# Zero-state products left out, a padded tile, stacked low-rank halves and a relaid instruction list in a three-branch decoder trunk

## Chip, cores and metric

The kernel runs on one core of one Trainium2 chip. The metric is the device time of one execution in microseconds (us), the median of several. Before the change three runs took 2274.77 to 2276.88 us, with a median of 2276.57 us.

## What is computed

A decoder trunk with 2 layers, a width of 1024 and 1024 tokens, in float32. Each layer makes one wide input projection, feeds three token mixers from it (pooling, retention, RWKV-7), projects each mixer's output, merges the three by gates, and projects once more:

```python
def hybrid_layer(x, c_act, positions, ...):
    mod = c_act @ w_ada + b_ada
    shift, scale, gate = jnp.split(mod[:, None, :], 3, axis=-1)
    h = rms_norm(x, norm_g) * (1.0 + scale) + shift
    proj = h @ w_in
    ...
    o_pool = causal_pool_mixer(pool_u, pool_w, pool_scale) * jax.nn.silu(pool_g)
    o_ret = retention(q, k, v, positions, ret_norm_g) * jax.nn.silu(ret_g)
    o_rwkv = rwkv7_time_mix(rw, ...) * jax.nn.silu(rw_g)
    branches = jnp.stack([o_pool, o_ret, o_rwkv], axis=2)
    y = jnp.einsum('btnw,nwd->btnd', branches, w_branch)
    gates = jax.nn.sigmoid(gate_logits.reshape(B, T, N_BRANCHES, D))
    merged = jnp.sum(gates * y, axis=2)
    return x + gate * (merged @ w_out)
```

Two mixers carry a state that starts at zero, and both need two low-rank or recurrent steps that matter here:

```python
def rwkv7_time_mix(p, shift_mu, w0, w2, a0, a2, ...):
    ...
    w = -jax.nn.softplus(-(w0 + jnp.tanh(wl) @ w2)) - 0.5
    a = jax.nn.sigmoid(a0 + al @ a2)
    ...
    def step(S, inp):
        r_t, w_t, k_t, v_t, a_t, b_t = inp
        sa = jnp.einsum('bhvk,bhk->bhv', S, a_t)
        S = (S * w_t[:, :, None, :] + sa[..., None] * b_t[:, :, None, :]
             + v_t[..., None] * k_t[:, :, None, :])
        return S, jnp.einsum('bhvk,bhk->bhv', S, r_t)
    _, y = lax.scan(step, jnp.zeros((B, H, N, N), jnp.float32), xs)

def retention(q, k, v, positions, ret_norm_g):
    ...
    def step(R, kv_n):
        return chunk_decay * R + kv_n, R
    _, R_prev = lax.scan(step, jnp.zeros((B, H, dh, dh), jnp.float32), jnp.moveaxis(kv, 2, 0))
```

Here `wl` and `al` are 64 wide and `w2`, `a2` are 64x512.

## The kernel before

All activations lie with channels on the 128 partitions and tokens along the free dimension, in two halves `h` of 512 tokens. A projection tile of 128 channels is 8 blocks of contraction. Each float32 operand is split into a high part that the fast matmul type (F32R) holds exactly and the low rest, and each block is three products: high times high, high times low, low times high (`mm1`). These products, 128x128 weights by 512 columns, go to PSUM tiles named `acc` and make up most of the program; I call them ordinary products. Plain float32 products (state, scores, transposes) are issued in two passes, transposes in one.

**The RWKV mixer** (`rwkv_task`) runs once per layer and pair of heads: 8 tasks, one after the other. A task treats 1024 tokens as 16 chunks of 64. `prepare` makes the scaled keys and queries for each half. It begins with the low-rank products (`lora_mm`, PSUM tiles `lw`): `tanh(wl) @ w2` uses partitions 0 to 63 of both operands and `al @ a2` partitions 64 to 127, each as three products of a high and a low part, so six products over 64 rows each. Their weights `lw` are loaded and split once per layer (`lora_load`), their moving operands `lt` once per half by the evacuation of the `lora` item (`evac_`). `scores` transposes the keys of each chunk (`bt` to `BKt`) and makes the score blocks `G` (PSUM tiles `g` and `two`); `states` makes `AV` (PSUM tile `av`); `invert` and `blocks` invert the unit triangular parts on DVE and in 32x32 products (`m1`, printed as `m`, and `two`). Then the loop over 16 chunks runs, and each step depends on the one before:

1. `two<-S,AR`: the state times the chunk's queries and keys; DVE adds `AV` and writes `xst`; ACT scales the state to `SP`.
2. `ch<-xst,G`: two products with 64 columns of data; the weight is 65 columns of `G`, where the last unit of the tile has only 64 left. ACT copies the result to `Z`.
3. `ch<-Z,BKt`: the update; DVE forms the next state `Sn` from it and `SP`, 64x64 per head.
4. `two<-Z,G`: the chunk's output, copied to `y` by ACT.

**The retention mixer** (`ret_task`) runs once per layer and head: 8 tasks of two halves, each with 4 blocks of 128 tokens. It makes scores (`rs`), transposes keys and values (`rkt`, `rvt`), makes the block products (`rkv`) and from them on DVE the running state `R`, and the output (`ro`).

**The order.** The program is not issued as it is written. Every call is recorded (`Log.call`), with a lane and a place; `Log.plan` then lays out a list for each engine. It goes through time, takes the engine that is free first, and among the operations that are ready by then the one with the smallest key (the place in the recording plus a bias per lane; RWKV has -3000). `pe_time` and `times` give each operation's length, and a few constants the extra length on PE: `SWITCH` (86 ns) when an ordinary product follows another kind, and `RESHAPE` (100 ns) when the rows of the weight or the half of output partitions differ from the product before. A tile of a ring of buffers is handed out in the order of the recording. `nc.emit` issues the list, so every instruction in the profile has the one line L543, and groups are told apart by their tiles. TensorE (PE), DVE, ACT, POOL (GpSimd) and SP's DMA queue each run their list in order.

Of the kernel before, what the change touches and what calls it, by code (L numbers as in the profile page):

```python
# [111 lines left out]
HOLD = 3000  # L112
SWITCH = 86
SEED = 0
SHAKE = 0
SIDE = 0.6
RESHAPE = 100
RATE = 0.0027
# [86 lines left out]
class Log:  # L205
# [75 lines left out]
    def pe_time(self, n, a, k):  # L281
        out = a[0]
        w = a[1] if n == "transpose" else k["lhsT"]
        f = out.free_size()
        if n != "transpose" and k["rhs"].dtype == F32R:
            t = 228 if f > 256 else 120
        else:
            t = 426 if f == 1 else (max(f * 0.846, w.free_size() * 0.8) + 3) * (1 if n == "transpose" else 2)
        return t / 2 if w.partition_size() == 64 and out.partition_size() == P else t

    def times(self, o):
        o.port = False
        n = max(x.free_size() for x in o.outs + o.ins_)
        if o.eng == "PE":
            occ = sum(self.pe_time(q, a, k) for _, a, k, q in o.calls)
# [41 lines left out]
    def plan(self):  # L337
# [102 lines left out]
        burst = None  # L440
        spell, was, shape = 0, False, None
        while len(done) < len(todo):
# [114 lines left out]
def trunk_kernel(ctx, tc, xT, cvec, pos, vecs, consts, w_ada, w_all, pool_w, lora_w, out):  # L557
# [7 lines left out]
    wp = pool("wp", 2)  # L565
    gp = pool("gp", 1)
    rp = pool("rp", 4)
    tp = pool("tp", 4)
    mp = pool("mp", 4)
    sb = pool("sb", 1)  # L570
# [8 lines left out]
    def gtile(s):  # L579
        return gp.tile([P, 32 * P], F32, tag="G", name=nm(s))  # L580

# [629 lines left out]
    def ret_task(l, hd, qT, kT, vT, sg):  # L1211
# [6 lines left out]
        for h in range(2):  # L1218
# [14 lines left out]
            kt = mo("rkt")  # L1233
            nc.scalar.activation(kt, ps, AF.Copy, scale=tl)
            yield 900
# [10 lines left out]
            with nc.together():  # L1246
                for c in range(4):
                    mmul(cl(kv, c), lhsT=cl(kt, c), rhs=cl(vt, c), start=True, stop=True)
            R = []
            for c in range(4):  # L1250
                R.append(prev)
                nx = sb.tile([P, P], F32, tag="R", name=nm("R"), bufs=4)
# [35 lines left out]
    def rwkv_task(l, hp, kT, rT, vp, lt, lw):  # L1288
        hc = slice(hp * P, (hp + 1) * P)
# [3 lines left out]
        G = Gf.rearrange("p (u n) -> p u n", n=P)  # L1293
        qa = lambda b: slice(64 + 32 * b, 96 + 32 * b)
# [8 lines left out]
        def prepare(h):  # L1303
            cr = slice(8 * h, 8 * h + 8)
            yield wait(*lt[h])
            pss = [mx("lw"), mx("lw")]
            lora_mm(pss, lw, hc, lt[h])
            sg = t_ri("sg")
# [84 lines left out]
        def scores(h):  # L1393
            yield max(until(whole[h] + 1000), wait(Z, spare=600))
            for q in range(2):
                ps = mx("bt")
                c0 = 8 * h + 4 * q
                with nc.together():
                    for c in range(4):
                        trans(ps[:, c * P : (c + 1) * P], jt(BK, slice(0, P), c0 + c), timed=True)  # L1400
                nc.scalar.copy(BKt[:, c0 : c0 + 4, :], ps.rearrange("p (c n) -> p c n", n=P))
                yield 1300
# [114 lines left out]
        for c in range(16):  # L1517
# [4 lines left out]
            S, Sn = SS[par], SS[1 - par]  # L1522
            pcc = pc[:, c : c + 1]
            SP = sb.tile([P, P], F32, tag="SP", name=nm("SP"), bufs=1)
            nc.scalar.activation(SP, S, AF.Copy, scale=pcc)
# [5 lines left out]
            if c > 1:  # L1531
                sa.own_dep = yout[-2]
            nc.vector.tensor_tensor(xst[0:64, :], cy[64:128, 0:P], AV[:, c * P : (c + 1) * P], op=ALU.add)
# [10 lines left out]
            for hd in range(2):  # L1544
                rw = slice(64 * hd, 64 * hd + 64)
                nc.vector.scalar_tensor_tensor(
                    Sn[rw, rw], ch[rw, P + 64 * hd : P + 64 * hd + 64], pc[rw, c : c + 1], SP[rw, rw],
                    op0=ALU.mult, op1=ALU.add,
                )
            yield 500  # L1550
            for hd in range(2):
# [4 lines left out]
                    Z[:, c, cols],  # L1556
                    start=False,
                    skip_group_check=True,
# [54 lines left out]
    def enter_layer(l):  # L1613
        nonlocal L_
        rope[:] = [None, None, None]
        L_ = (l, {}, {}, [])
        L_[3].extend(lora_load(l))

    def lora_load(l):
        raw = wp.tile([P, W], F32, tag="wr", name=nm("lraw"), bufs=3)  # L1620
        nc.sync.dma_start(out=raw, in_=lora_w[l])
        lw = [cp.tile([P, W], F32R, tag=f"lw{j}", name=nm("lw")) for j in range(2)]
        split(raw, *lw, nc.vector)
        return lw
# [10 lines left out]
    def evac_(item, ps, h):  # L1635
        l, st, ams, lw = L_
        kind = item[0]
        if kind == "lora":
# [4 lines left out]
            st.setdefault("lt", [None, None])[h] = r  # L1643
            split(d, *r, nc.vector)
        elif kind in ("k", "r", "v"):
# [8 lines left out]
            if kind == "v" and h == 1:  # L1654
                st[("task", i)] = rwkv_task(l, i, st[("k", i)], st[("r", i)], st[("v", i)], st["lt"], lw)
                add("rwkv", st[("task", i)])
# [263 lines left out]
    add("st", store_all([(hd[0][kt, h], xin[h][kt]) for h in range(2) for kt in range(8)]))  # L1920
    L_ = (0, {}, {}, [])
    L_[3].extend(lora_load(0))
    for i in range(3):
# [376 lines left out]
def _pack(inputs):  # L2300
# [78 lines left out]
    arr["pool_w"] = np.ascontiguousarray(f("pool_w"))  # L2379
    arr["lora_w"] = np.ascontiguousarray(np.concatenate([f("rwkv_w2"), f("rwkv_a2")], axis=1))  # L2380
    return arr
# [22 lines left out]
```

## Time and profile before

| What | Value |
|---|---|
| timed runs | 2274.77, 2276.57, 2276.88 us |
| median | 2276.57 us |
| span of the profiled execution | 2272.5 us |
| PE matmul instructions | 13076 |
| DVE, ACT, POOL instructions | 2776, 1795, 552 |
| mean DMA rate | 110 GB/s |

The span is the profiled execution's own time, from its first to its last instruction; the timed runs also hold what lies around it. How to read the rows in the prediction: in a list by time the first two numbers are start and length in us, "out<-in" are tiles by name, "128*65" are the rows and columns of the weight in use, "128x512" the result, and "x4" the number of instructions merged in the row. A matmul's length is its way through the array and not the time that it takes from the next one, so the distance between starts is what counts. In group rows the numbers behind the bar are busy us and mean ns of one, then the idle time before. In rows of one tile, three numbers are the shortest, median and longest ns of one.

### The profile page before, as it was taken

The numbers are of one execution on the slowest core, as the hardware profiler recorded it, in microseconds if no ns is written. First come the engines' busy times: TensorE is split into PE (matmuls) and PEld (weight loads), VectorE is DVE, ScalarE is ACT, GpSimd is POOL, SyncE is SP. The second block draws the span as 40 slices with busy tenths as digits, with TensorE's granted clock in tenths as the row PEclk, the third lists the DMA queues.
The fourth block names the chain that finished last, engine by engine and source line by source line (L and its number), as shares of the span: only waits on it lengthen the run. The fifth ranks groups of instructions, "written<-read, shape, count | busy, mean of one in ns | idle before, by whom it ended". The sixth has DMA issues, their size and how long they took to land.

```text
span 2272.5 us, 35073 instructions
## 1 busy us (share of the span) xinstructions
PE 2243.5 (99%) x13076; PEld 1865.8 (82%) x13076; DVE 1612.3 (71%) x2776; ACT 934.5 (41%) x1795; POOL 629.1 (28%) x552
## 2 busy tenths in 40 slices
PE   7999999999999999999999999999999999999998
PEld 6788888888888888888888888888888888888888
DVE  7997786867878765677677678687785744465854
ACT  5644434434244334323454444344433444441243
POOL 2223323322326221331232232333431500041211
PEclk9999999999999999999999999999999999999999
DMA  9212111112236563654531111111112533256442
GB/s 323 70 56 68 33 47 39 52 43 62 89 112 228 195 216 112 228 191 165 174 129 38 38 38 35 56 43 48 53 62 84 190 117 112 88 181 217 134 130 84
DMA packets 138042, 248.85 MB, mean 110 GB/s; under 512 B 15632, under 2 KB 18960, under 8 KB 137872
## 3 DMA queue, kind: packets, MB, share of 16 engines
q1 hardware_dynamic: 137872, 246.61, 33.2%
q8 instruction: 103, 1.69, 0.3%
q14 instruction: 67, 0.55, 0.1%
HBM read 187.04 MB, written 59.51 MB: 108 GB/s over the span
## 4 chain that ended last, share of the span: by engine, by line
PE 90%; DVE 7%; ACT 1%; issue 1%; DMA 0%; POOL 0%; DVEq 0%; ACTq 0%; POOLq 0%
PE acc L543 74%; PE two L543 3%; PE ch L543 2%; PE g L543 1%; PE av L543 1%; PE ro L543 1%; DVE ksq L543 1%; PE m L543 1%; PE bt L543 1%; PE lw L543 1%; PE rkv L543 1%; PE rs L543 1%; DVE ada_ps L543 0%; DVE G L543 0%; PE pps L543 0%
## 5 line engine op out<-in xcount | busy, mean ns | idle before, releaser
L543 PE MATMUL acc<-hhi,wh 128*128 128x512 f32 x1488 | 597.9, 402 | 0.0
L543 PE MATMUL acc<-hhi,wl 128*128 128x512 f32 x1488 | 596.9, 401 | 0.0
L543 PE MATMUL acc<-hlo,wh 128*128 128x512 f32 x1488 | 596.2, 401 | 0.0
L543 POOL TENSOR_TENSOR wl<-wr,wh 128x512 fp32r<-128x512 f32 x167 | 225.4, 1351 | 568.0 <-ACT wh L543 421.8
L543 PEld LDWEIGHTS acc<-hhi,wh 128*128 128x128 f32 x1488 | 280.6, 189 | 49.8 <-issue 1.8
L543 PEld LDWEIGHTS acc<-hlo,wh 128*128 128x128 f32 x1488 | 280.5, 189 | 49.3 <-issue 1.1
L543 PEld LDWEIGHTS acc<-hhi,wl 128*128 128x128 f32 x1488 | 280.4, 188 | 49.4 <-issue 0.7
L543 ACT CAST wh<-wr 128x512 fp32r<-128x512 f32 x242 | 149.3, 617 | 265.7 <-PE acc L543 204.7
L543 PE MATMUL acc<-T,wh 128*128 128x512 f32 x576 | 178.2, 390 | 0.0
L543 DVE SCALAR_TENSOR_TENSOR S<-ch,pc,SP 64x64 f32<-64x64 f32 x256 | 72.2, 282 | 87.1 <-PE ch L543 84.0
L543 PEld LDWEIGHTS acc<-T,wh 128*128 128x128 f32 x576 | 108.0, 188 | 22.4
L543 PE MATMUL acc<-T,wl 128*128 128x512 f32 x288 | 112.4, 390 | 0.0
L543 DVE TENSOR_TENSOR wl<-wsum,wh 128x512 fp32r<-128x512 f32 x69 | 49.2, 712 | 81.8 <-ACT wh L543 81.5
L543 ACT CAST wh<-wsum 128x512 fp32r<-128x512 f32 x96 | 59.5, 620 | 95.0 <-PE acc L543 92.9
L543 POOL TENSOR_TENSOR oz<-ol,oz 128x512 fp32r<-128x512 f32 x10 | 14.0, 1401 | 281.7 <-DVE wl L543 212.6
L543 DVE TENSOR_TENSOR xst<-two,MT 64x128 f32<-64x128 f32 x128 | 37.6, 293 | 68.4 <-PE two L543 47.7
L543 DVE TENSOR_TENSOR two<-two,tm 64x30 f32<-64x30 f32 (+14 forms) x240 | 78.9, 329 | 7.3
L543 ACT COPY Z<-ch 64x128 f32<-64x128 f32 x128 | 33.0, 258 | 123.3 <-PE ch L543 123.2
L543 DVE TENSOR_TENSOR tm<-MT,two 64x30 f32<-64x30 f32 (+14 forms) x240 | 76.3, 318 | 10.2 <-ACT two L543 3.4
L543 PE MATMUL acc<-oy,wh 128*128 128x512 f32 x256 | 80.1, 394 | 0.0
L543 PE MATMUL acc<-oz,wh 128*128 128x512 f32 x256 | 79.0, 389 | 0.0
L543 PE MATMUL acc<-oG,wh 128*128 128x512 f32 x256 | 78.9, 389 | 0.0
(329 smaller groups left out, 4890.3 us busy)
## 6 DMA issues: line engine op xcount, KB each, us to landing
wr<-in_w_all SPq DMA_DIRECT2D x268, 256.0 KB, 2.6
wraw<-in_w_all SPq DMA_DIRECT2D x96, 256.0 KB, 2.8
gd<-gsg SPq DMA_DIRECT2D x96, 256.0 KB, 2.0
gs<-gd SPq DMA_DIRECT2D x96, 256.0 KB, 3.5
wada<-in_w_ada SPq DMA_DIRECT2D x80, 256.0 KB, 3.4
ol<-od SPq DMA_DIRECT2D x48, 256.0 KB, 3.3
traw<-hd SPq DMA_DIRECT2D x32, 256.0 KB, 3.1
x<-in_xT SPq DMA_DIRECT2D x16, 256.0 KB, 4.9
```

Of the source, the lines that this page charges most:

```text
L543: o.inst = f(*a, **k)
```

## The change

Four things are changed.

- **Zero and unused state.** Chunk 0 of an RWKV task leaves out `two<-S,AR` and the scaled state, copies `AV` to `xst` instead of adding to it, and starts its output in `two` afresh. Chunk 15 leaves out the update, the scaled state, and the transpose of its keys. Retention leaves out the last block's key transpose and product in the second half, and the state that would follow.
- **Padded tile.** `G` has 16 more columns, the first of which a GpSimd memset clears in each task, so that the last unit can use 65 columns like the others. Its pool is opened later among the pools.
- **Low-rank products.** The high and low halves are stacked on the partitions: tile `r[0]` holds the high part of `tanh(wl)` on partitions 0 to 63 and its low part on 64 to 127, tile `r[1]` the same of `al` with the halves exchanged. The weights are laid out in DRAM twice over, for each head pair, and split into high and low columns. Each result is then two products over 128 rows. The weights are loaded in each task, from a ring with two tiles, the raw ones through the ring `mo`.
- **The list.** The extra lengths on PE are now: entering a form with 64 rows 250 ns, with 32 rows 122, any other change of form 200; 50 ns where a result narrower than 128 columns is followed by a weight or operand of 128 or more. The length of a product with one column is 224 ns outside of the lead-in.

```diff
-SWITCH = 86
+SHORT = 50
-RESHAPE = 100
+ENTER = {64: 250, 32: 122}
+LEAVE = 200
...
-                if o.big and not was:
-                    o.occ += SWITCH
-                    o.dur += SWITCH
-                was = o.big
                 rows = (o.ins_[0].partition_size(), o.outs[0].partition_size() > 64)
+                more = 0
                 if rows != shape:
-                    o.occ += RESHAPE
-                    o.dur += RESHAPE
+                    more = ENTER.get(rows[0], LEAVE)
+                elif was < 128 <= o.ins_[0].free_size():
+                    more = SHORT
+                o.occ += more
+                o.dur += more
+                was = o.outs[0].free_size()
...
-        return gp.tile([P, 32 * P], F32, tag="G", name=nm(s))
+        return gp.tile([P, 32 * P + 16], F32, tag="G", name=nm(s))
...
+            nkv = 4 - h
             with nc.together():
-                for c in range(4):
+                for c in range(nkv):
                     trans(cl(ps, c), cl(kT[h], c))
...
-    def lora_mm(pss, lw, hc, lt):
+    def lora_mm(pss, lw, lt):
         with nc.together():
-            for i, (a, b) in enumerate(((0, 0), (0, 1), (1, 0))):
-                for j in range(2):
-                    own = slice(64 * j, 64 * j + 64)
-                    mmul(pss[j], lw[a][own, hc], lt[b][own, :], start=(i == 0), stop=(i == 2))
+            for j in range(2):
+                for i in range(2):
+                    o = (2 * i + j) * P
+                    mmul(pss[j], lw[:, o : o + P], lt[j], start=(i == 0), stop=(i == 1))
...
+        nc.gpsimd.memset(Gf[:, 32 * P : 32 * P + 1], 0.0)
...
-                        n = min(65, 32 * P - u0)
+                        n = 65
...
-            sa = mmul(cy[:, 0:P], jt(AR, slice(0, P), c), S)
-            if c:
+            if c == 0:
+                nc.scalar.copy(xst[0:64, :], AV[:, 0:P])
+            else:
+                if c < 15:
+                    SP = sb.tile([P, P], F32, tag="SP", name=nm("SP"), bufs=1)
+                    nc.scalar.activation(SP, S, AF.Copy, scale=pc[:, c : c + 1])
+                sa = mmul(cy[:, 0:P], jt(AR, slice(0, P), c), S)
...
-                n = min(65, 32 * P - u0 - 64)
+                n = 65
...
-            mmul(ch[:, P : 2 * P], BKt[:, c, :], Z[:, c, :])
+            if c < 15:
+                mmul(ch[:, P : 2 * P], BKt[:, c, :], Z[:, c, :])
...
+    def lora_load(l, hp):
+        raw = mo("lraw")[:, 0 : 2 * P]
+        nc.sync.dma_start(out=raw, in_=lora_w[l, hp])
+        lw = cp.tile([P, W], F32R, tag="lw", name=nm("lw"), bufs=2)
+        split(raw, lw[:, 0 : 2 * P], lw[:, 2 * P : W], nc.vector)
         return lw
...
-            split(d, *r, nc.vector)
+            for j in range(2):
+                a, b = slice(64 * j, 64 * j + 64), slice(64 - 64 * j, 128 - 64 * j)
+                nc.scalar.copy(r[j][a, :], d[a, :])
+                nc.vector.tensor_tensor(r[j][b, :], d[a, :], r[j][a, :].bitcast(F32), op=ALU.subtract)
```

How the change moves instructions, first on PE around the first low-rank block of layer 0, near the end of the lead-in (`lw` is the PSUM tile on the left and the weights on the right, `lt` the moving operand, `acc` an ordinary product). Before:

```order
L543 MATMUL acc_258<-hlo_185,wbig_226 128x512
L543 MATMUL acc_258<-hhi_184,wbig_226 128x512
L543 MATMUL lw_271<-lt_240,lw_236 128x512
L543 MATMUL lw_272<-lt_240,lw_236 128x512
L543 MATMUL lw_271<-lt_241,lw_236 128x512
L543 MATMUL lw_272<-lt_241,lw_236 128x512
L543 MATMUL lw_271<-lt_240,lw_237 128x512
L543 MATMUL lw_272<-lt_240,lw_237 128x512
L543 MATMUL acc_258<-hhi_200,wbig_226 128x512
```

and with the change:

```order
L548 MATMUL acc_255<-hhi_184,wbig_226 128x512
L548 MATMUL acc_255<-hhi_200,wbig_226 128x512
L548 MATMUL acc_255<-hlo_201,wbig_226 128x512
L548 MATMUL lw_270<-lt_237,lw_263 128x512 x2
L548 MATMUL lw_271<-lt_238,lw_263 128x512 x2
L548 MATMUL acc_255<-hhi_200,wbig_226 128x512
L548 MATMUL acc_256<-hhi_194,wbig_226 128x512
```

Six products become four, one result after the other instead of in turn, and two ordinary products that stood behind the block now stand ahead of it.

The second place is PE at the last chunk of the first RWKV task (`ch`, `two`, `Z`, `G`, `BKt`, `xst` as in the four steps above). Before, with the 64-column weight in the second row, and the next task's low-rank block in between:

```order
L543 MATMUL ch_502<-xst,G_267 65x64
L543 MATMUL ch_502<-xst,G_267 64x64
L543 MATMUL acc_485<-hhi_202,wh_409 128x512
L543 MATMUL lw_546<-lt_247,lw_236 128x512
...
L543 MATMUL ch_502<-Z_269,BKt_268 128x128
L543 MATMUL two<-Z_269,G_267 65x64 x2
L543 MATMUL acc_485<-hlo_203,wh_409 128x512
```

and with the change:

```order
L548 MATMUL ch_499<-xst,G_266 65x64 x2
L548 MATMUL acc_486<-hhi_208,wh_408 128x512
L548 MATMUL acc_486<-hlo_209,wh_408 128x512
L548 MATMUL acc_486<-hhi_208,wl_409 128x512
L548 MATMUL acc_485<-hhi_216,wl_412 128x512
L548 MATMUL acc_485<-hhi_220,wh_411 128x512
L548 MATMUL acc_485<-hlo_221,wh_411 128x512
L548 MATMUL two<-Z_268,G_266 65x64 x2
```

The 64-column weight and the update are gone, and ordinary products stand between the remaining steps.

The third place is ACT, where the low-rank weights of the second task are cast (`lw<-lraw`), during the last chunks of the first task:

```order
L548 COPY Z_148_268<-ch_368_488 64x128
L548 CAST lw_385_505<-lraw_384_504 128x256
L548 COPY y_338_458<-two_93 64x128
L548 ACTIVATE SP_369_489<-S_284_404,pc_149_269 128x128
L548 ACTIVATE sg_394_514<-lw_392_512,vec0_100 128x512
L548 ACTIVATE aT_395_515<-lw_393_513,vec0_100 128x512
```

Before, the weights of all four tasks of a layer were cast at its start, and no cast of them stands between the steps of a task; now one does in each task.

More of the change, by code (lines that the diff above doesn't have):

```diff
@@ L287, in pe_time @@
         else:
-            t = 426 if f == 1 else (max(f * 0.846, w.free_size() * 0.8) + 3) * (1 if n == "transpose" else 2)
+            t = (max(f * 0.846, w.free_size() * 0.8) + 3 + 2 * (f == 64)) * (1 if n == "transpose" else 2)
+            if f == 1:
+                t = 426 if self.lead else 224
         return t / 2 if w.partition_size() == 64 and out.partition_size() == P else t
@@ L294, in times @@
         if o.eng == "PE":
+            self.lead = o.lane == "lead"
             occ = sum(self.pe_time(q, a, k) for _, a, k, q in o.calls)
@@ L1246, in ret_task @@
             with nc.together():
-                for c in range(4):
+                for c in range(nkv):
                     mmul(cl(kv, c), lhsT=cl(kt, c), rhs=cl(vt, c), start=True, stop=True)
@@ L1251, in ret_task @@
                 R.append(prev)
+                if c == nkv:
+                    break
                 nx = sb.tile([P, P], F32, tag="R", name=nm("R"), bufs=4)
@@ L1397, in scores @@
                 c0 = 8 * h + 4 * q
+                n = min(4, 15 - c0)
                 with nc.together():
-                    for c in range(4):
+                    for c in range(n):
                         trans(ps[:, c * P : (c + 1) * P], jt(BK, slice(0, P), c0 + c), timed=True)
-                nc.scalar.copy(BKt[:, c0 : c0 + 4, :], ps.rearrange("p (c n) -> p c n", n=P))
+                nc.scalar.copy(BKt[:, c0 : c0 + n, :], ps[:, 0 : n * P].rearrange("p (c n) -> p c n", n=P))
                 yield 1300
@@ L1542, in rwkv_task @@
             yield wait(Z)
-            mmul(ch[:, P : 2 * P], BKt[:, c, :], Z[:, c, :])
-            for hd in range(2):
+            if c < 15:
+                mmul(ch[:, P : 2 * P], BKt[:, c, :], Z[:, c, :])
+            for hd in range(2 if c < 15 else 0):
                 rw = slice(64 * hd, 64 * hd + 64)
[L1546 to L1549, printed above, removed]
+                new = ch[rw, P + 64 * hd : P + 64 * hd + 64]
+                if c == 0:
+                    nc.vector.tensor_scalar_mul(Sn[rw, rw], new, pc[rw, 0:1])
+                else:
+                    nc.vector.scalar_tensor_tensor(
+                        Sn[rw, rw], new, pc[rw, c : c + 1], SP[rw, rw], op0=ALU.mult, op1=ALU.add
+                    )
             yield 500
@@ L1615, in enter_layer @@
         rope[:] = [None, None, None]
[L1616 to L1623, printed above, removed]
+        L_ = (l, {}, {})
+    def lora_load(l, hp):
[3 more added lines that the diff above has]
+        split(raw, lw[:, 0 : 2 * P], lw[:, 2 * P : W], nc.vector)
         return lw
@@ L2379, in _pack @@
     arr["pool_w"] = np.ascontiguousarray(f("pool_w"))
-    arr["lora_w"] = np.ascontiguousarray(np.concatenate([f("rwkv_w2"), f("rwkv_a2")], axis=1))
+    lw = np.stack([f("rwkv_w2"), f("rwkv_a2")], axis=2).reshape(L, 64, 2, 4, P).transpose(0, 3, 1, 2, 4)
+    arr["lora_w"] = np.ascontiguousarray(np.concatenate([lw, lw], axis=2).reshape(L, 4, P, 2 * P))
     return arr
```

34 lines of the change are left out of this document (15 added, 19 removed).

## The prediction

> **What bounds the kernel now.** I read the page first (engine shares, then the chain that ended last), then the busy time by stretch with the waits of PE, and last the rows in order of time around single steps. Of the page:
>
> ```profile
> span 2272.5 us, 35073 instructions
> PE 2243.5 (99%) x13076; PEld 1865.8 (82%) x13076; DVE 1612.3 (71%) x2776; ACT 934.5 (41%) x1795; POOL 629.1 (28%) x552
> PE 90%; DVE 7%; ACT 1%; issue 1%; DMA 0%; POOL 0%; DVEq 0%; ACTq 0%; POOLq 0%
> ```
>
> TensorE is busy for 2243.5 of 2272.5 us, and 90% of the chain that ended last is its own work. The next engine, DVE, has 29% of the span free. The busy time by stretch (the first number behind each stretch is its length, the next the PE time):
>
> ```profile
> 0.00:100.00 100.00, 85.34 (x400) 70.06 (x401) 83.86 (x153) 63.02 (x101) 28.31 (x37) 0.95 0.62 218
> 100.00:700.00 600.00, 596.57 (x4078) 495.39 (x4075) 469.71 (x916) 251.68 (x524) 193.65 (x177) 1.00 0.21 66
> 700.00:1150.00 450.00, 449.55 (x2019) 371.88 (x2018) 311.33 (x410) 168.26 (x288) 123.64 (x89) 1.00 0.56 185
> 1150.00:1760.00 610.00, 608.25 (x4126) 502.50 (x4125) 454.25 (x886) 257.70 (x539) 182.18 (x177) 1.00 0.18 54
> 1760.00:2240.00 480.00, 480.00 (x2269) 402.56 (x2267) 281.35 (x383) 185.20 (x324) 98.52 (x70) 1.00 0.44 144
> ```
>
> From 100 to 2240 us PE idles for 3.4 + 0.5 + 1.8 + 0 = 5.7 us, at a granted clock of 1.00. The other 23 us of idle time lie in the lead-in and the last 33 us, where the change removes nothing. The largest wait inside is small:
>
> ```profile
> PE two L543 <- DVE S L543: 1.2, 4, 0.4
> ```
>
> So whatever leaves PE shortens the kernel by its full length, and what leaves another engine hardly at all. A busy PE is not yet a PE at work, though: the ends of matmuls are modelled, so I measure costs from start to start. The unit is the product of 512 columns; from the first to the last of these two rows 21 of them start without a break:
>
> ```profile
> 1257.10 0.39 PE L543 MATMUL acc<-hhi,wl 128*128 128x512 f32 x1
> ...
> 1261.87 0.39 PE L543 MATMUL acc<-hhi,wh 128*128 128x512 f32 x1
> ```
>
> 4.77 us / 21 = **0.227 us** each. Every block below is priced as the time from its first start to a later start of an ordinary product, less 0.227 for each ordinary product between.
>
> **Part 1, products with a zero or unused state.** The first chunk of each of the 8 RWKV tasks (4 head pairs, 2 layers) no longer multiplies the zero state (two<-S,AR), and the last one no longer makes the next state (ch<-Z,BKt) nor transposes its keys (one of bt's). Each of the 8 retention tasks leaves out the transpose and the product of its last block (rkt, rkv). The rows:
>
> ```profile
> 170.04 0.38 PE L543 MATMUL two<-S,AR 128*128 128x128 f32 x2
> ...
> 171.19 0.40 PE L543 MATMUL acc<-hhi,wl 128*128 128x512 f32 x1
> ```
>
> ```profile
> 1493.31 1.05 PE L543 MATMUL rkv<-rvt,rkt 128*128 128x128 f32 x8
> 1494.12 0.48 PE L543 MATMUL acc<-hhi,wl 128*128 128x512 f32 x1
> 1494.43 0.40 PE L543 MATMUL acc<-hhi,wh 128*128 128x512 f32 x1
> ```
>
> ```profile
> 291.90 0.60 PE L543 MATMUL rvt<-cst,rv 128*128 128x128 f32 x4
> 292.25 0.47 PE L543 MATMUL acc<-hlo,wh 128*128 128x512 f32 x1
> 292.57 0.39 PE L543 MATMUL acc<-hhi,wl 128*128 128x512 f32 x1
> ```
>
> A state product with its surroundings: 171.19 - 170.04 - 4 x 0.227 = 0.24 us, times 8 = 1.9. Four products of 128 columns (two passes each): 1494.43 - 1493.31 - 0.227 = 0.89, so 0.22 each; 8 rkv and 8 ch<-Z,BKt make 3.6. Four transposes: 292.57 - 291.90 - 0.227 = 0.44, so 0.11 each; 16 make 1.8. Together **-7.3 us**. On DVE and ACT the part removes more than it adds (an ACT copy of xst stands for a DVE addition); I cost that at nothing, since PE has other products to run between the steps.
>
> **Part 2, the padded tile.** The last unit of G had 64 columns as a weight where all others have 65. The group rows, and the two places in order of time, the first with the 64-column pair among its four ch (a row of its own when asked for alone), the second an ordinary chunk:
>
> ```profile
> L543 PE MATMUL av<-Z,G 128*64 128x64 f32 x16 | 2.6, 246 | 0.0
> L543 PE MATMUL ch<-xst,G 128*64 128x64 f32 x16 | 2.6, 246 | 0.0
> ```
>
> ```profile
> 1335.97 0.54 PE L543 MATMUL ch<-xst,G 128*65 128x64 f32 x4
> 1336.44 0.50 PE L543 MATMUL acc<-hhi,wh 128*128 128x512 f32 x1
> ...
> 1337.02 0.39 PE L543 MATMUL acc<-hhi,wl 128*128 128x512 f32 x1
> ```
>
> ```profile
> 1336.19 0.33 PE L543 MATMUL ch<-xst,G 128*64 128x64 f32 x2
> ```
>
> ```profile
> 1307.07 0.40 PE L543 MATMUL ch<-xst,G 128*65 128x64 f32 x4
> ...
> 1307.82 0.39 PE L543 MATMUL acc<-hlo,wh 128*128 128x512 f32 x1
> ```
>
> Both stretches run from the first ch to the start of the third ordinary product behind it: 1.05 against 0.75 us. The change of form costs 0.30 us, though the work is the same. 16 such places (32 passes) make **-4.7 us**. Nothing is exposed for it: one GpSimd memset of one column per task, far ahead of its use.
>
> **Part 3, low-rank products.** Now six products over 64 rows, in three pairs that start together; then four over 128 rows, of the ordinary form. The block at the start of layer 1:
>
> ```profile
> 1169.25 0.39 PE L543 MATMUL acc<-hhi,wbig 128*128 128x512 f32 x1
> 1169.57 0.97 PE L543 MATMUL lw<-lt,lw 64*128 64x512 f32 x6
> 1170.46 0.50 PE L543 MATMUL acc<-hhi,wbig 128*128 128x512 f32 x1
> 1170.80 0.40 PE L543 MATMUL acc<-hlo,wbig 128*128 128x512 f32 x1
> 1171.04 0.62 PE L543 MATMUL acc<-hhi,wbig 128*128 128x512 f32 x2
> ```
>
> 1171.04 - 1169.25 - 3 x 0.227 = 1.11 us for what should be 0.68 in three pairs; 0.43 is the price of entering and leaving the form. Four ordinary products cost 4 x 0.227 = 0.91, so each of 16 blocks gains 0.20: **-3.2 us**.
>
> The Trainium skill speaks against this part: "TensorEngine Tiling (Array Packing)", section Performance Considerations, advises two row tiles where the contraction is at most 64. By that alone the new form loses 0.23 us x 16 = 3.6 us, and the sum below would be 8.4 instead of 15.2. The trace's 1.11 us decides for the change here, and the same page's Tiling Modes section, by which a change of mode drains TensorE, fits the 0.43.
>
> What the part adds: twice the casts and subtractions on the way from lora's evacuation to the products (they now stack the halves), and a load of weights for each task where one per layer did.
>
> ```profile
> L543 ACT CAST lt<-lt x4: 614/618/622, 74.4 to 1189.0; 128x512 fp32r<-128x512 f32 x4
> L543 DVE TENSOR_TENSOR lt<-lt,lt x4: 678/684/685, 75.1 to 1190.8; 128x512 fp32r<-128x512 f32 x4
> lraw<-in_lora_w SPq DMA_DIRECT2D x2, 256.0 KB, 2.9
> ```
>
> At worst a second cast and subtraction stand fully in the way four times: 4 x (0.62 + 0.68) = 5.2 us. At best nothing: counted in the order, the first block stands behind two more ordinary products than before (0.45 us), and the other blocks stand far behind the evacuation that makes their halves. I take nothing and keep 5 us for the range. A late load is a rival below. The loads go to SP's queue among the weights' own, at 0.18 to 0.21 DMA share in those stretches.
>
> **Part 4, the list.** New prices for changes of form move nearly every row, but not the number of dear things: the order has 25 entries into the 64-row form for the g products and 24 into the 32-row form, before and after, and mostly four ordinary products still stand between dependent steps of a chunk. So the work is the same and only waits can change. Nothing in the trace prices them but the waits there are: 5.7 us from 100 to 2240. The bounds are all of them gone (-5.7) and twice as many added (+11); I take zero, as the spacing between steps, which made them, is the same.
>
> **Sum.** 7.3 + 4.7 + 3.2 = **15.2 us** less. The profiled execution spans 2272.5, which becomes 2257.3. The timed median 2276.57 is 4.1 above that span; I leave that difference as it is: 2276.57 - 15.2 = **2261.4 us**. A measurement here can tell about 0.2%, 4.6 us, from no change, so the sum is three times that.
>
> **Rivals.**
> - The list gives part back: the new order meets two or three times today's waits. For it: every row moved, and the lead-in has 14.7 us of PE idle time that can grow as well. Against it: the same spacing. +4 to +11 us: 2265 to 2272.
> - The list also helps: planned times nearer to the true ones remove most waits. -4 us: 2257.5.
> - Pairs cost only their streaming (the page's rule): the block is 0.68 us, the change of form being hidden elsewhere. Sum 7.3 + 4.7 - 3.6 = 8.4: 2268.2. Against it: 1.11 us at a place without any wait.
> - The form does not go away with 65 columns: part 2 is void, 2266.1. Against it: the other units with 65 columns show none of it.
> - Slower: the weights for the low-rank products come late. Each task's first block waits for its own load, cast and subtraction, and PE runs in order, so all ordinary products behind the block wait too, as does the task's scan. From issue that is 2.9 + 0.6 + 0.7 = 4.2 us. If PE is always there at the issue, 8 x 4.2 = 33.6: 2276.6 - 15.2 + 33.6 = 2295. It decides against the change from 15.2 / 8 = 1.9 us per task. For it: the load takes a slot of a ring that is handed out in order, so it can't be issued far ahead. Against it: the list puts the block behind the load's due time, and has other products for PE.
>
> **How the numbers follow.** Forecast 0.72 (2261.4), list gives back 0.13, list helps 0.07, pairs 0.03, columns 0.02, late weights 0.03. Faster by over 0.2% is below 2272.0: all but the late weights (0.03) and the far end of the first rival (0.04): 0.93. Range: down to 2256 (all waits gone), up to 2269 (the 5 us of part 3's cover, or half of the first rival).
>
> **What would show it.** In the changed profile PE has 12980 instructions, 96 fewer; no row with 64*128 128x512 or 128*64; an lw block of four takes 0.91 us in order of time; a last chunk's ch block takes 0.75. PE's idle time from 100 to 2240 stays near 5.7 us. Wrong would be: lw among the waits of PE, long waits at lraw or lt, or an idle time of PE of over 10 us more.

## The result and the profile after

The changed kernel takes **2262.21 us** (median of 4 runs, 2261.42 to 2263.11) against 2276.35 us before (4 runs, 2274.77 to 2276.88), a ratio of 0.9939 with a 95% interval of 0.9927 to 0.9951. That is 14.1 us less. The forecast was 2261.4.

The page of the changed kernel, the lines that answer to those shown of before:

```profile
span 2260.6 us, 34881 instructions
PE 2229.0 (99%) x12980; PEld 1865.3 (83%) x12980; DVE 1589.5 (70%) x2750; ACT 931.5 (41%) x1795; POOL 627.0 (28%) x564
PE 89%; DVE 7%; ACT 2%; issue 1%; DMA 1%; SPq 0%; DVEq 0%; ACTq 0%
```

TensorE is still the bound, with 96 instructions fewer; DVE, ACT and POOL have hardly changed. The busy time by stretch (the columns are those of the prediction, so the PE time is the second number behind the stretch):

```profile
0.00:100.00 100.00, 83.77 (x353) 69.53 (x354) 83.14 (x150) 59.80 (x96) 27.45 (x39) 0.98 0.62 217
100.00:700.00 600.00, 596.82 (x4091) 499.33 (x4091) 473.11 (x912) 253.12 (x531) 193.33 (x181) 1.00 0.22 68
700.00:1150.00 450.00, 449.32 (x2022) 371.64 (x2021) 304.68 (x408) 169.06 (x289) 124.08 (x90) 1.00 0.57 185
1150.00:1760.00 610.00, 606.77 (x4113) 509.32 (x4111) 444.21 (x878) 257.60 (x534) 185.09 (x185) 1.00 0.18 56
1760.00:2240.00 480.00, 479.90 (x2314) 403.59 (x2313) 277.98 (x389) 187.83 (x337) 96.28 (x69) 1.00 0.44 143
```

From 100 to 2240 us PE idles for 3.2 + 0.7 + 3.2 + 0.1 = 7.2 us, 1.5 more than before; in the first 100 us it idles for 16.2, 1.5 more as well.

The two blocks whose price the prediction worked out, in order of time: a low-rank block, and the last chunk of the first RWKV task.

```profile
1341.56 1.07 PE L548 MATMUL lw<-lt,lw 128*128 128x512 f32 x4
1342.47 0.39 PE L548 MATMUL acc<-hhi,wl 128*128 128x512 f32 x1
```

```profile
240.98 0.40 PE L548 MATMUL ch<-xst,G 128*65 128x64 f32 x4
...
241.73 0.62 PE L548 MATMUL acc<-hhi,wl 128*128 128x512 f32 x2
```

The low-rank block lasts 1342.47 - 1341.56 = 0.91 us, and from the first `ch` to the third ordinary product behind it are 241.73 - 240.98 = 0.75 us. Both are the prices that the prediction set.

**Where time was given back.** Two places stand out. The first is the entry to layer 1, the longest wait of PE behind the lead-in. Rows of DVE and PE there, in order of time; the bracket gives the idle time of the engine before the row and what ended it:

```profile
1172.12 3.37 DVE L548 RECIPROCAL ksq<-ksq 128x256 f32<-128x256 f32 x2
1175.40 0.11 DVE L548 COPY pc<-sg 128x8 f32<-128x8 f32 x1
1175.42 0.68 DVE L548 TENSOR_TENSOR ka<-ka,k 128x512 f32<-128x512 f32 x1
1176.02 0.75 DVE L548 SCALAR_TENSOR_TENSOR ksq<-k,vec,ksq 128x512 f32<-128x512 f32 x1
1176.68 0.75 DVE L548 SCALAR_TENSOR_TENSOR r<-acc,omu,r 128x512 f32<-128x512 f32 x1
...
1177.48 0.50 PE L548 MATMUL acc<-hhi,wbig 128*128 128x512 f32 x1 [1.80 <-DVE r L548]
```

The next projection needs the PSUM tile that the `r` row empties, and 4.6 us of the task's DVE work (1172.12 to 1176.68) stand ahead of that row. PE stands for 1.80 us. This DVE work is not new: in the kernel before, the same five rows stand in the same order, the `r` row starts at 1180.84, 11.3 us after the low-rank block as it does here, and PE has no wait there. So the list changed the other side: before, PE had products to run until the `r` row was done, and here it comes to the product that needs the tile too early.

The second is the lead-in. The first low-rank block, in the kernel before and in the changed one:

```profile
6.04 7.13 PE L543 MATMUL sums<-fixed,sq 128*128 128x1 f32 x32 [6.04 <-DVE sq L543]
...
24.27 2.74 PE L543 MATMUL sums<-fixed,ringG 128*128 128x1 f32 x24
...
75.41 1.16 PE L543 MATMUL lw<-lt,lw 64*128 64x512 f32 x6
```

```profile
6.22 1.87 PE L548 MATMUL sums<-fixed,sq 128*128 128x1 f32 x8 [6.22 <-DVE sq L548]
8.89 5.28 PE L548 MATMUL sums<-fixed,sq 128*128 128x1 f32 x24 [0.80 <-DVE sq L548]
...
26.42 4.26 PE L548 MATMUL sums<-fixed,ringG 128*128 128x1 f32 x20
...
79.13 1.51 PE L548 MATMUL lw<-lt,lw 128*128 128x512 f32 x4
```

It starts 79.13 - 75.41 = 3.7 us later; two ordinary products that now stand ahead of it are 0.45 of that, and 3.3 remain. The busy time up to that block and behind it, before and with the change:

```profile
0.00:75.41 75.41, 61.54 (x269) 51.78 (x270) 60.50 (x119) 47.82 (x75) 24.77 (x34) 0.93 0.82 289
75.41:2272.50 2197.09, 2181.99 (x12808) 1813.99 (x12807) 1551.85 (x2658) 886.70 (x1721) 604.31 (x518) 1.00 0.32 103
```

```profile
0.00:79.13 79.13, 64.70 (x271) 54.64 (x271) 62.85 (x122) 47.89 (x76) 23.03 (x34) 0.98 0.79 273
79.13:2260.60 2181.47, 2164.32 (x12709) 1810.67 (x12709) 1526.60 (x2629) 883.65 (x1720) 603.93 (x530) 1.00 0.33 104
```

Up to the block PE idles for 13.9 us before and 14.4 with the change, only 0.6 more, although it now has a wait in the sums of squares over the input, which before went through without a break. The other 2.7 us are busy time: the same products stand further apart for longer. The sums over `ringG` are 0.11 us apart before (24 in 2.74 us) and 0.21 here (20 in 4.26). Ordinary products early in the lead-in are 0.43 us apart in both kernels, nearly double the 0.227 of later, and with the change the short distance begins 2 to 3 us later. A second trace of the changed kernel, taken for the experiments, has the block at 78.49 us, with 62.2 us busy and 16.3 idle, so two executions of one program already differ here.

From that block to the end of the span the profiled executions take 2197.1 and 2181.5 us, 15.6 less, or 15.2 without the two products that moved. By the profile, which models the ends of matmuls, PE's busy time there fell by 17.7 us and its idle time rose by 2.1.

### The profile page after: what moved, and what is told of

It is laid out like the page before. It is cut to its first block, busy times and chain, and to the rows that moved or that the text cites. A ratio compares the mean times of both kernels' runs of the same rounds, so it can differ in the third digit from the quotient of the medians.

```text
span 2260.6 us, 34881 instructions
## 1 busy us (share of the span) xinstructions
PE 2229.0 (99%) x12980; PEld 1865.3 (83%) x12980; DVE 1589.5 (70%) x2750; ACT 931.5 (41%) x1795; POOL 627.0 (28%) x564
## 4 chain that ended last, share of the span: by engine, by line
PE 89%; DVE 7%; ACT 2%; issue 1%; DMA 1%; SPq 0%; DVEq 0%; ACTq 0%
PE acc L548 73%; PE two L548 3%; PE ch L548 2%; PE ro L548 1%; PE g L548 1%; PE av L548 1%; DVE two L548 1%; DVE tm L548 1%; DVE ksq L548 1%; PE rs L548 1%; DVE G L548 1%; PE rkv L548 1%; PE m L548 1%; PE bt L548 1%; PE lw L548 1%
## 5 line engine op out<-in xcount | busy, mean ns | idle before, releaser
L548 DVE SCALAR_TENSOR_TENSOR S<-ch,pc,SP 64x64 f32<-64x64 f32 x224 | 63.3, 283 | 87.1 <-PE ch L548 84.3
L548 DVE TENSOR_TENSOR tm<-MT,two 64x30 f32<-64x30 f32 (+14 forms) x240 | 76.3, 318 | 11.4 <-ACT two L548 4.6
L548 DVE TENSOR_TENSOR wl<-wraw,wh 128x512 fp32r<-128x512 f32 x48 | 33.7, 703 | 63.5 <-ACT wh L548 63.5
```

The lines of the kernel that those rows point to most:

```text
L548: o.inst = f(*a, **k)
```

## Experiments

The theory, called A in the expectations, is the prediction's: TensorE is the bound, so an edit is worth the spacing of the products that it removes. The rivals are that the list which every edit brings about gives or takes as much, and that the products cost something else than their rows say; where an expectation names them B or C, it says what they are.

**Each part alone.** Four kernels, each the kernel before with one part of the change; the planner lays out a new list for each. On their chip the kernel before took 2275.89 us (28 runs).

```diff
+                for c in range(nkv):
                     trans(cl(ps, c), cl(kT[h], c))
...
+            if c == 0:
+                nc.scalar.copy(xst[0:64, :], AV[:, 0:P])
...
+            if c < 15:
+                mmul(ch[:, P : 2 * P], BKt[:, c, :], Z[:, c, :])
...
```

> The kernel of before with part 1 alone (zero and unused state left out). Theory A, PE's own time sets the end and each part is worth what its instructions take there: 7.3 us less than before, 2269. Rival B, what a part saves is mostly lost or made in the list that it gives rise to, since every variant is laid out anew: anything from 3 to 11 us less, and not the sum in the end. PE idle from 100 to 2240 us near 5.7 by A, off by several us by B.

Measured: 2267.49 us, ratio 0.9966 (0.9954 to 0.9978), so 8.4 less. PE idles for 6.4 us from 100 to 2240, near the 5.7 of theory A.

```diff
-        return gp.tile([P, 32 * P], F32, tag="G", name=nm(s))
+        return gp.tile([P, 32 * P + 16], F32, tag="G", name=nm(s))
...
+        nc.gpsimd.memset(Gf[:, 32 * P : 32 * P + 1], 0.0)
...
-                n = min(65, 32 * P - u0 - 64)
+                n = 65
```

> Before with part 2 alone (65 columns for G's last unit). A: 16 changes of form at 0.30 us are gone, 4.7 us less, 2271.7; a last chunk's ch block takes 0.75 us in place of 1.05. Rival: the form did not cost it, the place did (end of a task): 0 to 1 us less.

Measured: 2274.87 us, ratio 0.9997 (0.9988 to 1.0006), 1.0 less. That is the rival's number, but its reason does not hold. The same last chunk as in the prediction, in this kernel:

```profile
1338.33 0.40 PE L543 MATMUL ch<-xst,G 128*65 128x64 f32 x4
...
1339.08 0.40 PE L543 MATMUL acc<-hhi,wl 128*128 128x512 f32 x1
```

From the first `ch` to the third ordinary product behind it are 0.75 us, where before they were 1.05: the form cost it, and not the place. Added up from start to start over the trace from the first low-rank block on, idle time left out, the `ch` and `av` products take 4.2 us less than before. The new list gives it back elsewhere: PE idles for 6.8 us from 100 to 2240, 1.1 more, and other products (`g`, `m`, ordinary ones) stand further apart; why was not followed.

```diff
-    def lora_mm(pss, lw, hc, lt):
+    def lora_mm(pss, lw, lt):
...
+            for j in range(2):
+                for i in range(2):
+                    o = (2 * i + j) * P
+                    mmul(pss[j], lw[:, o : o + P], lt[j], start=(i == 0), stop=(i == 1))
...
```

> Before with part 3 alone (four low-rank products over 128 rows, weights loaded per task). A: 16 blocks at 0.91 for 1.11 us, 3.2 us less, 2273.2. Rival, pairs cost only their streaming: 3.6 us more, 2280. Rival, the longer way of lt and the late weights stand in PE's way: up to 5 us more than A, 2278, with waits at lw, lt or the tiles of the evacuation behind them.

Measured: 2277.53 us, ratio 1.0008 (0.9999 to 1.0016), 1.6 more.

```diff
-RESHAPE = 100
+ENTER = {64: 250, 32: 122}
+LEAVE = 200
...
```

> Before with part 4 alone (new prices in the list, the same instructions). A: the same work, 0 +- 3 us, 2273 to 2280, PE instructions 13076. Rival, true prices remove the waits: 4 to 6 us less. Rival, the new order meets more waits: 4 to 11 us more.

Measured: 2278.95 us, ratio 1.0012 (1.0003 to 1.0021), 3.1 more.

The four differences add up to 8.4 + 1.0 - 1.6 - 3.1 = 4.7 us less, where all four together gave 14.1. Two expectations missed by 3.7 and 4.8 us. The rows above show where the second kernel's gain went. For the third its busy time and three rows of PE show a part:

```profile
100.00:700.00 600.00, 594.15 (x4079) 495.35 (x4078) 466.28 (x918) 250.00 (x526) 191.24 (x176) 1.00 0.21 64
...
1150.00:1760.00 610.00, 607.72 (x4082) 506.06 (x4081) 443.99 (x877) 257.63 (x532) 186.21 (x181) 1.00 0.18 56
```

```profile
233.74 0.49 PE L543 MATMUL two<-S,AR 128*128 128x128 f32 x2 [1.16 <-DVE S L543]
...
318.00 1.19 PE L543 MATMUL m<-MT,G 32*32 32x32 f32 x32 [0.83 <-DVE MT L543]
...
431.54 0.47 PE L543 MATMUL bon<-rkh,bone 128*128 128x512 f32 x1 [1.02 <-DVE G L543]
```

PE idles for 5.9 us in the first of these stretches and 2.3 in the second; with the two stretches that aren't shown it is 8.6 from 100 to 2240, 3.0 more than before, of the 4.8 that are missing. None of the three rows is a low-rank product: most of the gain was eaten by waits of other steps in a list laid out anew. In the fourth kernel PE idles 3.4 more than before between 100 and 2240 (9.0 us), about as much as it lost. So such a run does not price its edit. The next ones hold the order.

**With the list held.** Each of these undoes one part in the changed kernel. For the first two, the planner's prices were set so that every engine issues in the changed kernel's order; the third takes back the prices alone. The changed kernel ran beside them: before 2275.29 us (9 runs).

> The changed kernel once more, as the measure for the next three on the same chip: 2262 +- 1 us by every theory.

Measured: the changed kernel 2261.79 us, ratio 0.9941 (0.9928 to 0.9953).

```diff
-                        n = 65
+                        n = min(65, 32 * P - u0)
...
-                n = 65
+                n = min(65, 32 * P - u0 - 64)
```

> The changed kernel with 64 columns again for G's last unit, and the list held fixed: every engine's instructions stand in the order of the changed kernel. Theory A, the form costs PE 0.30 us at each of 16 places whatever the list: 4.7 us more than the changed kernel, 2267. Rival, part 2 is worth the 1 us that it gave alone: 2263.

Measured: 2266.65 us, ratio 0.9962 (0.9950 to 0.9975), 4.9 above the changed kernel. The groups with 64 columns are back and the same place in the first task takes longer:

```profile
241.50 0.54 PE L549 MATMUL ch<-xst,G 128*65 128x64 f32 x4
...
242.54 0.62 PE L549 MATMUL acc<-hhi,wl 128*128 128x512 f32 x2
```

(The row merges the two shapes under the first one's name.) 242.54 - 241.50 = 1.04 us against the 0.75 above. Part 2 was worth its 4.7. The slowest of the five runs of the changed kernel (2264.05) is faster than the fastest here (2266.19).

```diff
-            for j in range(2):
-                for i in range(2):
-                    o = (2 * i + j) * P
-                    mmul(pss[j], lw[:, o : o + P], lt[j], start=(i == 0), stop=(i == 1))
+            for i, (a, b) in enumerate(((0, 0), (0, 1), (1, 0))):
+                for j in range(2):
+                    own = slice(64 * j, 64 * j + 64)
+                    o = (2 * a + j) * P
+                    mmul(pss[j], lw[own, o : o + P], lt[j ^ b][own, :], start=(i == 0), stop=(i == 2))
```

> The changed kernel with six low-rank products over 64 rows in three pairs, from the stacked tiles, and the list held fixed. (The product of the high weights and the low input reads the other input's low part, so that small term is not the reference's.) Theory A: 16 blocks at 1.11 for 0.91 us, 3.2 us more than the changed kernel, 2265.4. Rival, pairs cost only their streaming: 3.6 us less, 2258.6. Rival, part 3 is worth what it gave alone: 1.6 us less, 2260.6.

Measured: 2264.70 us, ratio 0.9953 (0.9940 to 0.9965), 2.9 above the changed kernel. A block of this kernel:

```profile
1342.90 0.39 PE L550 MATMUL acc<-hlo,wh 128*128 128x512 f32 x1
1343.22 0.96 PE L550 MATMUL lw<-lt,lw 64*128 64x512 f32 x6
1344.11 0.50 PE L550 MATMUL acc<-hhi,wl 128*128 128x512 f32 x1
1344.45 0.40 PE L550 MATMUL acc<-hhi,wh 128*128 128x512 f32 x1
1344.68 0.39 PE L550 MATMUL acc<-hlo,wh 128*128 128x512 f32 x1
```

Up to the last start are 1344.68 - 1342.90 = 1.78 us, less 3 x 0.227 for the ordinary products 1.10. A change of form shows on both sides: 0.32 us from the last ordinary product to the block and 0.34 from the first one behind it to the next, where 0.23 is usual. The three pairs alone would be 0.68. The Trainium skill, "TensorEngine Tiling (Array Packing)", section Performance Considerations, names two row tiles for a contraction of at most 64. By that alone the pairs would be 3.6 us better over 16 blocks, an estimate from the 0.68 and the 0.91; here they are 2.9 worse, as each block pays for entering and leaving the form. The Trainium skill's section Tiling Modes on the same page says that a change of mode drains TensorE, which fits these rows; it gives no price. The five runs do not overlap with those of the changed kernel, but only just (2264.13 against 2264.05).

```diff
-ENTER = {64: 250, 32: 122}
-LEAVE = 200
+RESHAPE = 100
...
```

> The changed kernel with the old prices in the list, parts 1 to 3 kept. Theory A, the list is worth nothing in itself: 2262 +- 3. Rival, the new prices are worth something once the other parts are there, though alone they cost 3 us: 2265 or more. Rival, they cost 3 us here too: 2259.

Measured: 2262.00 us, ratio 0.9941 (0.9927 to 0.9954), 0.2 above the changed kernel. Beside the other three parts the new prices are worth nothing, though alone they cost 3.1. By the traces (one each) it is two small effects that cancel: behind the first low-rank block PE is busy for 0.9 us less with the new prices (2164.3 against 2165.2) and idle for 0.7 more (17.2 against 16.5).

**The zero-state products put back.** At or next to their old places in TensorE's order 40 products were added, whose results nothing reads (the state products write to `ch` in place of `two`); the rest of the change stays. Before took 2275.98 us on this chip (15 runs).

```diff
+                if (c, hd) == (0, 0):
+                    again(tc.nc.tensor.matmul, ch[:, 2 * P : 3 * P], lhsT=jt(AR, slice(0, P), c), rhs=S, start=True, stop=True)
+                if (c, hd) == (15, 1):
+                    again(tc.nc.tensor.matmul, ch[:, P : 2 * P], lhsT=BKt[:, 14, :], rhs=Z[:, 14, :], start=True, stop=True)
...
```

> The changed kernel with 40 products put back at their old places on TensorE, 8 each of two<-S,AR style (written as ch<-S,AR), ch<-Z,BKt, rkv<-rvt,rkt, and of the transposes in bt and rkt; the order of all other instructions on every engine is that of the changed kernel. Nothing reads the results of the 40, so the output is the same. Theory A (they cost what their rows say, as PE has no gaps): 1.8 us for the 16 transposes, 3.6 for 16 products of 128 columns, and about 0.2 each for the 8 state products, together 7.1 to 7.3 us over the changed kernel: 2268.9 to 2269.1 where that takes 2261.8. Rival B (part of the 8.4 us that the part alone gave is its own list): clearly less than 7, by 2 us or more. Rival C (the steps around them on DVE and ACT were what cost): under 2 us over the changed kernel, since those stay left out here.

Measured: 2273.15 us, ratio 0.9990 (0.9982 to 0.9999). That is 11.4 above the 2261.79, or 10.7 when both are taken against the kernel before on their own chip; more than any of the three expected. The profile shows what came on top: waits on ACT that the changed kernel has not, 3.0 us together, all around the last chunk of a task of layer 0.

```profile
241.67 0.66 PE L549 MATMUL rkt<-cst,rk 128*128 128x128 f32 x4 [1.26 <-ACT Z L549]
...
389.69 0.65 PE L549 MATMUL rvt<-cst,rv 128*128 128x128 f32 x4 [0.52 <-ACT Z L549]
...
533.51 1.16 PE L549 MATMUL rs<-rq,rk 128*128 128x128 f32 x8 [1.26 <-ACT Z L549]
```

Just ahead of each, ACT copies values into the `Z` of the next task, and here starts that copy only after the last state product. PE idles for 10.6 us from 100 to 2240, 3.4 more than in the changed kernel. 10.7 to 11.4 less 3.4 is 7.3 to 8.0 us for the 40 products, beside the 7.1 to 7.3 of theory A. Without a subtraction it comes out the same: added up from start to start, idle time left out, the rows of `ch`, `rkv`, `rkt` and `bt` take 7.4 us more than in the changed kernel, and these are the tiles of all 40. So the products cost what their rows say, and rivals B and C fall; the timed 11.4 is that and the waits. The run holds the order, but it does not hold the waits: the copy into `Z` shows that a product which nobody reads can still keep another engine. Why the copy is released later was not followed further.

**Three shuffles of the list.** The changed kernel with the same work; the keys outside the lead-in and the RWKV lanes are moved a little, and the planner lays out the list with them.

```diff
-SEED = 0
-SHAKE = 0
+SEED = 1
+SHAKE = 40
```

> The changed kernel with its list laid out anew: the keys of the operations outside of the RWKV and lead-in lanes are moved by up to 20 places, first shuffle. The same instructions in another order. Theory B (each list meets its own waits of a few us): some 1 to 4 us from the changed kernel's 2261.8, of either sign, with the difference in PE's idle time. Theory A (the order does not matter, only the work does): within 0.7 us of it.

> As the first shuffle, with another seed: by theory B 1 to 4 us from 2261.8, of either sign; by theory A within 0.7 us.

> As the first shuffle, with a third seed: by theory B 1 to 4 us from 2261.8, of either sign, and the three differ from each other by as much; by theory A within 0.7 us.

Measured, in the same order: 2261.85 us (ratio 0.9938, 0.9925 to 0.9952), 2265.36 (0.9955, 0.9943 to 0.9968) and 2261.65 (0.9935, 0.9923 to 0.9948). Two are where the changed kernel is, one is 3.5 to 3.7 us above them; none is faster by what could be told. So the scatter is real, but smaller than expected for two of three, and none of the three shows the changed kernel's list to be a lucky one. About half of what the slow one loses shows as idle time of PE between 100 and 2240 (8.9 us against 7.2). The entry to layer 1 alone has 3.2 us of it, where the changed kernel has 1.8:

```profile
1165.15 0.70 PE L548 MATMUL lw<-lt,lw 128*128 128x512 f32 x2 [0.42 <-DVE lt L548]
1166.47 0.70 PE L548 MATMUL lw<-lt,lw 128*128 128x512 f32 x2 [0.61 <-DVE xres L548]
...
1178.37 0.47 PE L548 MATMUL acc<-hhi,wbig 128*128 128x512 f32 x1 [2.13 <-DVE r L548]
```

The first row is the danger that the prediction kept 5 us for: the low-rank block waits for the stacked halves of `lt`. It is 0.42 us here, and in the changed kernel it does not show.

The other half follows just behind the third of these waits. For 3.4 us the granted clock is half:

```profile
1179.70:1183.10 3.40, 3.40 (x10) 2.64 (x9) 3.07 (x5) 0.00 (x0) 2.38 (x3) 0.51 0.00 0
```

Ordinary products stand 0.43 us apart there in place of 0.227, so by estimate it costs 3.4 x (1 - 0.227 / 0.43) = 1.6 us. The changed kernel has no such stretch behind its 1.80 us. The third shuffle has one as well (1176.7 to 1180.1, behind a wait of 2.12) and is not slower for it as a whole; the first has none behind a wait of 2.1. So a stretch at half clock can follow a wait at this place, but it does not do so each time, and what brings it about was not tested.

## Why the prediction was right, and where it was off

- **The bound.** Right. TensorE is the bound in every kernel run, and the work that left it came out of the time. That the change removes nothing in the lead-in is not quite so: two of the 16 low-rank blocks lie in its 100 us (75.41 and 94.20 before).
- **Part 1, 7.3 us.** Shown in size: 7.4 by the rows of the products that were put back, or 7.3 to 8.0 from the timed run with the added waits taken off. The timed run itself has 10.7 to 11.4, and the part alone, in a list of its own, 8.4.
- **Part 2, 4.7 us.** Shown: 4.9 with the list held.
- **Part 3, 3.2 us.** Shown: 2.9 with the list held. The longer way through casts and subtractions, taken at nothing, seems to show in one block, the first one in the lead-in, whose row is 1.51 us long where the one quoted from layer 1 has 1.07; no later block is among the waits of PE.
- **Part 4, nothing.** Right beside the other parts (0.2), wrong for the part alone (3.1 more). The reason given, that the spacing between steps is the same, does not hold in general: the shuffles and the parts alone leave the spacing rules alone, and three of these kernels are 3.5 to 4.8 us from what they were expected to take. That the zero came out is in part luck.
- **The sum.** 4.9 + 2.9 + 7.3 to 8.0 = 15.1 to 15.8, against 15.2; with the waits that the run with the products put back added, it would be 18.5 to 19.2. The timed 14.1 falls short of the forecast by 1.1, and the repeated run, with 13.5, by 1.7. The interval of the first, 11.2 to 16.6 us, holds 15.2 as well, so the shortfall is not clear of noise. By the traces two errors of about 2 us cancel behind the first low-rank block: the busy time there fell by 17.2 (17.7 less the two products that moved), 2.0 more than the three parts are priced at, and the idle time rose by 2.1, where the prediction had neither. The second is the first rival in small; it had named the lead-in too, and the first low-rank block starts later.
- **The span and the median.** The prediction left the 4.1 us between the span of before and its median as they were. In every other run on record the time is 1.7 to 1.9 us above the span, so the profiled execution of before was some 2 us faster than its median. It was also faster than any of 52 further executions of the kernel before on three chips, whose spans go from 2272.7 to 2276.0 us, with medians of 2273.5 to 2274.2. Against its span the forecast was 2257.3 and the result 2260.6, 3.3 too low; against the medians only 0.8. So 1 to 2 us of that 3.3 belong to a fast execution of before and not to the change. Whether they lie in the lead-in, which grew by 3.3 us too, one trace of before can't show.
- **The rivals.** That pairs cost only their streaming fell with the low-rank run (2.9 more, not 3.6 less). That the form does not go away with 65 columns fell with the padded-tile run. That the list helps (its sum comes to 2257.4, not 2257.5) fell: PE idles more, and the old prices take the same time. That the weights come late fell: behind the lead-in no `lw` row of the changed kernel is among PE's waits.

## What to carry to other kernels

Where one engine is busy for 99% of the span, the spacing of its instructions, measured from start to start at one place and multiplied, priced two edits of 3 and 5 us to 0.3 us in 2260, and the third to within 1 once the waits were taken off. A scheduler that lays out a new list for each variant moved the time by up to 4.8 us against the prices, so a part of a change that is timed alone can read as nothing or as a loss; hold the order, or undo the part in the final kernel, before you drop it. Look first at a stage's entry, at a product that needs a tile emptied by another engine: that is where the new list put its longest wait. Compare both engines' rows with those of before, since the work ahead of the evacuation may be the same and only the product come earlier. And ask how the traced execution compares with the timed ones: the trace of before was faster than every other execution on record.

## What the runs showed of the hardware that was not expected

The kernel with the padded tile alone has the same PE order as the kernel before far into the lead-in, and yet its first low-rank block starts 1.9 us later:

```profile
6.06 1.87 PE L543 MATMUL sums<-fixed,sq 128*128 128x1 f32 x8 [6.06 <-DVE sq L543]
6.68 2.09 ACT L543 ACTIVATE sq<-x 128x512 f32<-128x512 f32 x3 [1.40 <-DMA x<-in_xT]
8.77 5.28 PE L543 MATMUL sums<-fixed,sq 128*128 128x1 f32 x24 [0.84 <-DVE sq L543]
...
25.19 5.11 PE L543 MATMUL sums<-fixed,ringG 128*128 128x1 f32 x24
...
77.33 1.16 PE L543 MATMUL lw<-lt,lw 64*128 64x512 f32 x6
```

ACT waits 1.40 us for an input tile to land, where no such wait of the kernel before is over 0.33:

```profile
6.48 0.63 ACT L543 ACTIVATE sq<-x 128x512 f32<-128x512 f32 x1 [0.33 <-DMA x<-in_xT]
```

Of the 14 profiled executions only two, that of before and that of the zero-state part alone, have the 32 sums without a break; in the others the second tile or a later one comes too late, by 0.16 to 0.98 us on PE, whatever the list. The landing of the first loads thus differs between executions or between built programs.

The wait is less than half of the 1.9 us. Up to its first low-rank block this kernel idles less on PE than before (13.0 us against 13.9) and is busy for longer (64.4 against 61.5): the same 24 sums over `ringG` take 5.11 us here and 2.74 in the kernel before, 0.21 against 0.11 each. So what starts late also runs slowly for longer. That the late tile brings the slow stretch about was not tested. Executions of one program differ as well: both traces of the changed kernel have the late second tile, and one has its slow sums and the other a wait in their place, 0.6 us apart at the block. How much of the 1.9 us is due to the built program was not settled: it would take several traces of the kernel before.
